# Seven of eleven gate/up panels of a SwiGLU layer with half their contraction by Strassen's block products

## The chip, the cores and the metric

The kernel runs on one core of one Trainium2 chip. The metric is the device time of one execution in microseconds (us), lower is better. The kernel before takes 2181.07 us, the median of three runs (2180.75, 2181.07, 2186.59). Engines are named as in the profile: PE is TensorE's matmuls and PEld its weight loads, DVE is VectorE, ACT is ScalarE, POOL is GpSimd, SP is SyncE, whose queue issues the DMAs.

## What is computed

A trunk of two layers over 256 tokens of width 2048, in float32. Each layer has a mixer (layer 0: a linear recurrence beside spatial gating; layer 1: stick-breaking attention beside pooling) and a SwiGLU feed-forward part, each followed by a LayerNorm, with scales, shifts and gates that come from a conditioning vector c (adaLN). What matters here is the feed-forward part of layer 1:

```python
D_FF = 5632
def swiglu(h, w_gate, w_up, w_down):
    return (jax.nn.silu(h @ w_gate) * (h @ w_up)) @ w_down
...
h = x * (1.0 + scale2) + shift2
ffn_out = swiglu(h, ffn_w_gate[layer], ffn_w_up[layer], ffn_w_down[layer])
x = layer_norm(ALPHA * x + (1.0 + gate2) * ffn_out, norm_g[layer, 1], norm_b[layer, 1])
```

## The kernel before, in words

The 256 tokens are two blocks of 128 (`tb`). The contraction over 2048 is cut into four chunks of 512 (`ch`), each of four k-tiles of 128. The 5632 columns of gate and up are cut into eleven panels of 512. A weight is a tile of 128 x 2048 numbers (1 MB): one chunk of the contraction, one panel, gate or up. `load_raw` (line 139) loads it on SP's queue into one of four raw buffers named w.

Products are made at nearly full float32 precision from two parts. `split` (line 81) lets ACT write the upper part h (line 84, a copy that rounds) and DVE the lower part l = w - h (line 85), in halves of 128 x 1024; h and l have four buffers each, so two weights. The activations xs are split in the same way, once, into xh and xl (four chunks of 128 x 4 x 256). `products` (line 154) then runs three matmuls of 512 columns per k-tile: xh h, xh l and xl h (lines 161 to 163). A weight thus gives 2 blocks x 4 k-tiles x 3 = 24 matmuls, and a half gives 12. They add up in PSUM banks named acc, of which there are six; two more, aux, take transposes.

`linear` (line 181) goes through groups of weights: for each group over the chunks, for each chunk over the group's weights, loading, splitting and multiplying. In `ffn` (line 384) a group is one panel with its gate and its up, so a panel takes 8 weights and four banks, and after the last chunk `evac_gu` (line 393) lets ACT take silu of the gate's bank (line 398) and DVE multiply it by the up's bank (line 406); the product is transposed on PE (line 228) and copied into hid by ACT or DVE (line 412). In layer 1 all eleven panels run like that. After each of the first four groups `resid` prepares a part of the residual on DVE (`residual`, lines 370 to 376) from rows of norm_g and norm_b that lie in the row buffers rg and rb, one buffer each. Then `rows` (line 231) loads the rows of the layer's last LayerNorm into the same buffers, `gate_rows` (line 240) spreads the gate, and the down-projection runs, a `linear` over hid, whose chunks are split as they come (xh, xl), and w_down.

After each weight `linear` calls a pump. It issues work of the adaLN terms that are still to come: a pump of rate 0.2 issues a unit at each fifth call. A unit is a load of 1 MB into one of the four raw buffers and two DVE instructions of 128 x 1024 that multiply and add up (`ada_dot`, line 94, line 99). In the feed-forward part of layer 1 the pump named last has rate 0.2 and 16 units.

No order is written out by hand here. A scheduler orders the instructions of each engine when the kernel is built, by their place in the program and by when they can start, and a tile waits for a free buffer of its name; on the chip each engine then runs its instructions in that order.

Of the kernel before, what the change touches and what calls it, by code (L numbers as in the profile page):

```python
# [10 lines left out]
ALU = mybir.AluOpType  # L11
# [17 lines left out]
RAW_GA = (0, 1)  # L29
RAW_OUT = (0, 1)  # L30
PAD = 16

_VEC = {}
_off = 0
# [8 lines left out]
def trunk_kernel(ctx, tc, I, out):  # L43
# [134 lines left out]
    def acc_bank():  # L178
        return psum["acc"].tile([P, NB], F32, name="acc")

    def linear(groups, chunks, wsrc, stat, evac, after=None, pump=None, opened=None, close=None,
               raw=None):
        ng, nch = len(groups), len(chunks)
        total = ng * nch
        for gi, group in enumerate(groups):
            banks = opened if gi == 0 and opened is not None else {}
            for ci, ch in enumerate(chunks):
                first, last = ci == 0, ci == nch - 1
                left = total - gi * nch - ci
                if first and banks:  # L190
                    if last:
                        for tb in range(2):
                            for nb in group:
                                evac(nb, tb, banks[nb, tb])
                    continue
                if close is not None and left == QUIET and pump is not None:
                    drain(pump.gen)
                st = stat(gi, ch)
                if close is not None and left == 1:
                    close(group, {nb: load_w(wsrc(nb, ch)) for nb in group}, banks, st, evac)  # L200
                    break
                for nb in group:
                    xr = raw(gi, ci, nb) if raw is not None else None
                    hl = load_w(wsrc(nb, ch)) if xr is None else load_raw(wsrc(nb, ch))
                    flush(mark["v"])
                    for hf in range(2):
                        for tb in range(2):
                            if first and hf == 0:
                                banks[nb, tb] = acc_bank()
                            if xr is None:  # L210
                                products(banks[nb, tb], st, hl, tb, (hf,), first, last)
                            else:
                                products32(banks[nb, tb], xr, hl, tb, (hf,), first, last)
                    if last:
                        for tb in range(2):
                            evac(nb, tb, banks[nb, tb])
                    if pump is not None and not (close is not None and left <= QUIET):
                        pump()
            if after is not None:
                after(gi)  # L220
# [4 lines left out]
    def transposed(src, n):  # L225
        pt = psum["aux"].tile([P, n, P], F32, name="aux")
        for i in range(n):
            T.transpose(pt[:, i], src[:, i * P:(i + 1) * P], ident)  # L228
        return pt

    def rows(l, s):
        rg = p_row.tile([P, D], F32, name="rg")
        nc.sync.dma_start(rg, I["norm_g"][l, s:s + 1, :].partition_broadcast(P))
        rb = p_row.tile([P, D], F32, name="rb")
        nc.sync.dma_start(rb, I["norm_b"][l, s:s + 1, :].partition_broadcast(P))
        return rg, rb
# [141 lines left out]
    def ffn_src(l):  # L378
# [2 lines left out]
            return (I["wu"] if up else I["wg"])[l, pan, ch]  # L381
        return src

    def ffn(l, ln, resid, x, pump, passes, finish):
        xs = ln["xs"]
        with tc.tile_pool(name=f"hid{l}", bufs=1) as p_hid:
            hid = p_hid.tile([P, FF // P, S], F32, name="hid")
            sil = {}

            def slot(pan):  # L390
                return pan if passes is None else (pan - 1) % NPAN

            def evac_gu(nb, tb, bk, part=None):
                pan, up = divmod(nb, 2)
                if not up:
                    sg = p_t.tile([P, NB], F32, name=f"sg{tb}")
                    if part is None:
                        A.activation(sg, bk, AF.Silu)
                    else:
                        V.tensor_tensor(sg, part, bk, op=ALU.add)  # L400
                        A.activation(sg, sg, AF.Silu)
                    sil[tb] = sg
                    return
                sg = sil[tb]
                if part is None:
                    V.tensor_tensor(sg, sg, bk, op=ALU.mult)
                else:
                    V.tensor_tensor(part, part, bk, op=ALU.add)
                    V.tensor_tensor(sg, sg, part, op=ALU.mult)
                pt = transposed(sg, 4)  # L410
                h0 = 4 * slot(pan)
                nc.any.tensor_copy(hid[:, h0:h0 + 4, tb * P:(tb + 1) * P], pt)

            src = ffn_src(l)
            p0 = 0
            if passes is not None:
                p0 = 5
                groups = [(2 * p, 2 * p + 1) for p in range(p0)]

                def part(nb, tb):  # L420
                    return hid[:, 4 * nb + 2 * tb:4 * nb + 2 * tb + 2].rearrange("p a b -> p (a b)")

                def stash(nb, tb, bk):
                    A.activation(part(nb, tb), bk, AF.Copy)

                def add(nb, tb, bk):
                    V.tensor_tensor(part(nb, tb), part(nb, tb), bk, op=ALU.add)  # L427

                def final(nb, tb, bk):
                    evac_gu(nb, tb, bk, part(nb, tb))  # L430

                for ch in range(4):
                    linear(groups, (ch,), src, lambda gi, c: xs[c], (stash, add, add, final)[ch],
                           pump=passes[ch] if ch < 3 else pump, opened=ln["banks"] if ch == 0 else None)
                    if ch < 3:
                        drain_all(passes[ch])
            linear([(2 * p, 2 * p + 1) for p in range(p0, NPAN)], range(4), src, lambda gi, ch: xs[ch], evac_gu,
                   after=lambda gi: resid(gi) if gi < 4 else None, pump=pump,
                   opened=ln["banks"] if p0 == 0 else None)
            rg, rb = rows(l, 1)  # L440
            gate_rows(l, 1)
            stats = [p_t.tile([P, 4, 6], F32, name=f"st{tb}") for tb in range(2)]
            res, close = finish(stats, rg, rb)
            linear([(0, 1), (2, 3)], range(NPAN), lambda nb, ch: I["wd"][l, nb, ch],
                   lambda gi, ch: xs_split(hid[:, 4 * slot(ch):4 * slot(ch) + 4]), make_resid(x, (l, 1), stats),
                   pump=pump, close=close)
        return res
# [467 lines left out]
```

## Time and profile before

| | |
|---|---|
| time, median of three runs | 2181.07 us |
| span of the profiled execution | 2175.9 us |
| median less span | 5.2 us |
| PE, DVE, ACT busy, share of the span | 97%, 74%, 44% |
| feed-forward part of layer 1, panels 4 to 10 | 1607 to 1919 us |

The profile is of one execution. It shows the span from its first instruction to its last; of the profiled execution itself no other time is given, and the runs' times, taken without a profile, lie about 5 us above the span. Busy times add up the instructions' durations; those of matmuls are modelled and overlap, and so do the ends of DVE's instructions by some hundredths of a microsecond. In rows of groups, "L85 DVE TENSOR_TENSOR l<-w,h 128x1024 ... x113" are the instructions of line 85 on DVE that read tiles w and h and write tile l. In a timeline, "[1.50 <-ACT h L84]" says that the engine stood idle for 1.50 us before, until line 84's writing of h on ACT released it.

### The profile page before, as it was taken

To read this page: it belongs to the slowest core of one execution; us is meant where nothing else is said; L and a number is where in the kernel's file an instruction comes from. 1 tells how busy PE (TensorE), PEld (TensorE's weight loads), DVE (VectorE), ACT (ScalarE), POOL (GpSimd) and SP (SyncE) were. 2 spreads that over 40 slices of the span, in tenths; PEclk is the share of its full clock that TensorE was granted. 3 is DMA by queue.
4 is the path that set the end of the run, shared out by engine and by line. 5 is a ranking of instruction groups with operands and counts; after the bars stand their busy time and mean duration, and the time that the engine had idled before them with its cause. 6 is when DMAs were issued, how large, how long until landed. Compare 5 with 4: busy or idle time off the path is not lost.

```text
span 2175.9 us, 24074 instructions
## 1 busy us (share of the span) xinstructions
PE 2111.6 (97%) x9124; PEld 1666.4 (77%) x9124; DVE 1618.6 (74%) x2202; ACT 966.5 (44%) x1124; POOL 31.5 (1%) x55
## 2 busy tenths in 40 slices
PE   7989999999999999999999999999999999999996
PEld 3556767887888888888868777868888888888885
DVE  7778988899977788889779977666555555555656
ACT  1215733544544445444444556354444444444442
POOL 0000000000000000000000011000000000000000
PEclk9999999999999999999999999999999999999998
DMA  9987787988888888888858877646676666555552
GB/s 399 388 322 267 303 329 297 341 325 336 301 314 312 322 330 322 335 319 312 319 217 311 324 267 292 261 173 221 230 271 229 222 226 233 208 203 193 194 194 91
DMA packets 84747, 601.20 MB, mean 276 GB/s; under 512 B 9444, under 2 KB 9876, under 8 KB 13846
## 3 DMA queue, kind: packets, MB, share of 16 engines
q1 hardware_dynamic: 84630, 599.67, 73.7%
q8 instruction: 71, 1.16, 0.2%
q14 instruction: 46, 0.37, 0.1%
HBM read 597.51 MB, written 2.12 MB: 276 GB/s over the span
## 4 chain that ended last, share of the span: by engine, by line
PE 85%; DVE 9%; ACT 2%; DMA 2%; issue 1%; POOL 1%; SPq 0%; DVEq 0%; ACTq 0%; POOLq 0%
PE acc L162 25%; PE acc L163 25%; PE acc L161 24%; DVE w L99 3%; PE hd L547 3%; PE acc L152 3%; DVE l L85 2%; PE aux L228 2%; DMA w<-in_ada_w 1%; PE hs L162 1%; PE hs L163 1%; PE hs L161 1%; DMA w<-in_w_cd 0%; ACT h L84 0%; POOL z L736 0%
## 5 line engine op out<-in xcount | busy, mean ns | idle before, releaser
L85 DVE TENSOR_TENSOR l<-w,h 128x1024 fp32r<-128x1024 f32 x676 | 822.9, 1223 | 421.4 <-ACT h L84 420.1
L84 ACT ACTIVATE h<-w 128x1024 fp32r<-128x1024 f32 x676 | 711.6, 1059 | 862.0 <-PE acc L163 689.4
L162 PE MATMUL acc<-l,xh 128*128 128x512 f32 x2608 | 1019.2, 391 | 6.2 <-DVE l L85 5.8
L161 PE MATMUL acc<-h,xh 128*128 128x512 f32 x2608 | 1018.2, 392 | 5.9 <-ACT xh L318 4.5
L163 PE MATMUL acc<-h,xl 128*128 128x512 f32 x2608 | 1018.3, 391 | 0.0
L162 PEld LDWEIGHTS acc<-l,xh 128*128 128x128 f32 x2608 | 489.8, 188 | 112.4 <-DVE l L85 11.8
L161 PEld LDWEIGHTS acc<-h,xh 128*128 128x128 f32 x2608 | 489.5, 188 | 108.2 <-ACT xh L318 5.5
L163 PEld LDWEIGHTS acc<-h,xl 128*128 128x128 f32 x2608 | 489.8, 188 | 100.4 <-DVE xl L319 0.3
L99 DVE SCALAR_TENSOR_TENSOR w<-w,silc 128x1024 f32<-128x1024 f32 x384 | 459.0, 1219 | 18.0 <-DMA w<-in_ada_w 15.6
L547 PE MATMUL hd<-w,y 128*128 128x512 f32 x192 | 93.8, 642 | 20.7 <-DVE y L545 20.7
L547 PEld LDWEIGHTS hd<-w,y 128*128 128x128 f32 x192 | 38.4, 205 | 72.7 <-issue 43.2
L85 DVE TENSOR_TENSOR xl<-hid,xh 128x1024 fp32r<-128x1024 f32 x44 | 53.9, 1224 | 34.2 <-ACT xh L84 33.6
L84 ACT ACTIVATE xh<-hid 128x1024 fp32r<-128x1024 f32 x44 | 46.8, 1063 | 63.0 <-PE acc L162 63.0
L152 PE MATMUL acc<-w,hx 128*128 128x512 f32 x96 | 43.1, 599 | 2.8 <-ACT hx L313 2.7
L161 PE MATMUL hs<-h,xh 128*128 128x512 f32 x96 | 40.9, 428 | 0.0
L162 PE MATMUL hs<-l,xh 128*128 128x512 f32 x96 | 39.0, 406 | 0.0
L163 PE MATMUL hs<-h,xl 128*128 128x512 f32 x96 | 38.0, 396 | 0.0
L84 ACT ACTIVATE xh<-y 128x1024 fp32r<-128x1024 f32 x12 | 12.7, 1058 | 56.6 <-DVE y L545 48.6
L152 PEld LDWEIGHTS acc<-w,hx 128*128 128x128 f32 x96 | 17.6, 190 | 23.4 <-issue 17.5
L99 DVE DVE_READ_ACCUMULATOR w<-w,silc 128x1 f32 x384 | 31.3, 82 | 0.0
L152 PE MATMUL acc<-w,y 128*128 128x512 f32 x64 | 28.5, 592 | 0.0
L427 DVE TENSOR_TENSOR hid<-hid,acc 128x512 f32<-128x512 f32 x40 | 27.2, 683 | 1.5 <-PE acc L163 1.4
(207 smaller groups left out, 851.4 us busy)
## 6 DMA issues: line engine op xcount, KB each, us to landing
w<-in_ada_w SPq DMA_DIRECT2D x192, 1024.0 KB, 5.1
w<-in_wg SPq DMA_DIRECT2D x88, 1024.0 KB, 5.2
w<-in_wu SPq DMA_DIRECT2D x88, 1024.0 KB, 5.1
w<-in_wd SPq DMA_DIRECT2D x88, 1024.0 KB, 4.9
w<-in_w_cd SPq DMA_DIRECT2D x32, 1024.0 KB, 6.2
w<-in_w_ab SPq DMA_DIRECT2D x20, 1024.0 KB, 5.2
w<-in_w_ab_out SPq DMA_DIRECT2D x16, 1024.0 KB, 7.0
w<-in_w_cd_out SPq DMA_DIRECT2D x16, 1024.0 KB, 6.7
```

Source lines behind the costliest of these rows:

```text
L84: A.activation(h, src, AF.Copy)
L85: mark["v"] = V.tensor_tensor(l, src, h, op=ALU.subtract)
L99: V.scalar_tensor_tensor(w[:, cs], w[:, cs], 1.0, silc[:, cs], op0=ALU.mult, op1=ALU.mult, accum_out=acc[:, hf:hf + 1])
L152: T.matmul(bk, x[:, k, ts], w[:, k], start=first and k == 0, stop=last and k == 3)
L161: T.matmul(bk, xh[:, k, ts], h[:, j], start=first and k == 0, stop=False)
L162: T.matmul(bk, xh[:, k, ts], l[:, j], start=False, stop=False)
L163: T.matmul(bk, xl[:, k, ts], h[:, j], start=False, stop=last and k == 3)
L228: T.transpose(pt[:, i], src[:, i * P:(i + 1) * P], ident)
L427: V.tensor_tensor(part(nb, tb), part(nb, tb), bk, op=ALU.add)
L547: T.matmul(banks[nb, tb], xt[:, k, tb * P:tb * P + P], w[:, i // 2], start=kb == 0, stop=kb == KB - 1)
```

## The change

Layer 1's panels 0 to 3 stay as they are (`FOLD = 4`). Panels 4 to 10 go to a new function `folded`. For chunks 0 and 1 it takes the two token blocks and two chunks as a 2 x 2 block matrix of x, and gate and up of the two chunks as a 2 x 2 block matrix of weights, and forms the four results with Strassen's seven block products (in Winograd's form) instead of eight. Block sums of x are made and split once, ahead of panel 4. Sums of weights are made in each panel by four DVE instructions of 128 x 2048 (`plus` and the sum into t), and each sum is split like a weight. Chunks 2 and 3 run as before (`plain`). Seven banks and partial results are joined by DVE sums of 128 x 512. One of the eight loads (b22) goes into the row buffer rb, t lies in the row buffer rg. `BY_DMA` is empty, so no sum is made by a DMA. The pump is called eight times per panel, as before.

```diff
+FOLD = 4
+BY_DMA = ()
...
+    def product(bk, st, hl, first, last=False):
+        xh, xl = st
+        for hf in range(2):
+            h, l = hl[hf]
+            for j in range(2):
+                k = 2 * hf + j
+                T.matmul(bk, xh[:, k], h[:, j], start=first and k == 0, stop=False)
+                T.matmul(bk, xh[:, k], l[:, j], start=False, stop=False)
+                T.matmul(bk, xl[:, k], h[:, j], start=False, stop=last and k == 3)
+
+    def folded(p_s, src, pans, xs, pump, emit):
...
+        sx = [p_s.tile([P, 3, CH, P], F32R, name=n) for n in ("sxh", "sxl")]
...
+        tmp = p_row.tile([P, 4, CH, P], F32, name="rg")
+        a21, a11, s, a = (tmp[:, i] for i in range(4))
+
+        def put(st, v):
+            A.activation(st[0], v, AF.Copy)
+            V.tensor_tensor(st[1], v, st[0], op=ALU.subtract)
+
+        x11, x12, x22 = view(0, t0), view(1, t0), view(1, t1)
+        s1, s2, s4, s3 = slot(0), slot(1), slot(2), view(0, t1)
+        V.tensor_tensor(a21, *s3, op=ALU.add)
+        V.tensor_tensor(a11, *x11, op=ALU.add)
+        V.tensor_tensor(a, *x22, op=ALU.add)
+        V.tensor_tensor(s, a21, a, op=ALU.subtract)
+        put(s1, s)
+        V.tensor_tensor(s, s, a11, op=ALU.subtract)
+        put(s2, s)
+        V.tensor_tensor(a, *x12, op=ALU.add)
+        V.tensor_tensor(a, a, s, op=ALU.add)
+        put(s4, a)
+        V.tensor_tensor(a21, a11, a21, op=ALU.subtract)
+        put(s3, a21)
...
+        def plain(bks, w, c, first, last):
+            hl = halves_of(w)
+            for hf in range(2):
+                for tb in range(2):
+                    opens = first[tb] if isinstance(first, tuple) else first
+                    products(bks[tb], xs[c], hl, tb, (hf,), opens, last)
+            pump()
...
+        for pan in pans:
+            g, u = 2 * pan, 2 * pan + 1
+            b11 = load_raw(src(g, 0))
+            b12 = load_raw(src(u, 0))
+            b22 = p_row.tile([P, 4, NB], F32, name="rb")
+            nc.sync.dma_start(b22, src(u, 1))
+            w11 = halves_of(b11)
+            m1 = acc_bank()
+            product(m1, x11, w11, True, True)
+            c11 = p_t.tile([P, NB], F32, name="sg0")
+            A.activation(c11, m1, AF.Copy)
+            t = p_row.tile([P, 4, NB], F32, name="rg")
+            V.tensor_tensor(t, b11, b12, op=ALU.add)
+            m5 = acc_bank()
+            product(m5, s1, halves_of(t), True, True)
+            pump()
+            plus("t2", t, b22, src(u, 1))
+            m6 = acc_bank()
+            product(m6, s2, halves_of(t), True, True)
+            c21 = p_t.tile([P, NB], F32, name="sg1")
+            V.tensor_tensor(c21, c11, m6, op=ALU.add)
+            c12 = t512()
+            V.tensor_tensor(c12, m5, c21, op=ALU.subtract)
+            be, bd = acc_bank(), acc_bank()
+            plain((be, bd), load_raw(src(u, 2)), 2, True, False)
+            b21 = load_raw(src(g, 1))
+            bb = acc_bank()
+            product(bb, x12, halves_of(b21), True)
+            pump()
+            plus("t3", b12, b22, src(u, 1))
+            m7 = acc_bank()
+            product(m7, s3, halves_of(b12), True, True)
+            V.tensor_tensor(c21, c21, m7, op=ALU.add)
+            c22 = t512()
+            V.tensor_tensor(c22, c12, m7, op=ALU.subtract)
+            ba = acc_bank()
+            plain((bb, ba), load_raw(src(g, 2)), 2, (False, True), False)
+            product(be, s4, halves_of(b22), False)
+            pump()
+            plus("t4", t, b21, src(g, 1))
+            plain((be, bd), load_raw(src(u, 3)), 3, False, True)
+            V.tensor_tensor(c12, c12, be, op=ALU.add)
+            V.tensor_tensor(c22, c22, bd, op=ALU.add)
+            product(ba, x22, halves_of(t), False)
+            pump()
+            plain((bb, ba), load_raw(src(g, 3)), 3, False, True)
+            for tb, (sg, up, bk) in enumerate(((c11, c12, bb), (c21, c22, ba))):
+                V.tensor_tensor(sg, sg, bk, op=ALU.add)
+                A.activation(sg, sg, AF.Silu)
+                V.tensor_tensor(sg, sg, up, op=ALU.mult)
+                emit(pan, tb, sg)
...
-            linear([(2 * p, 2 * p + 1) for p in range(p0, NPAN)], range(4), src, lambda gi, ch: xs[ch], evac_gu,
+            p1 = FOLD if l else NPAN
+            linear([(2 * p, 2 * p + 1) for p in range(p0, p1)], range(4), src, lambda gi, ch: xs[ch], evac_gu,
                    after=lambda gi: resid(gi) if gi < 4 else None, pump=pump,
                    opened=ln["banks"] if p0 == 0 else None)
+            if p1 < NPAN:
+                folded(p_hid, src, range(p1, NPAN), xs, pump, emit)
```

`halves_of` splits a weight as `load_w` does, `plus` is a sum of two tiles of 128 x 2048 on DVE, and `emit` is the transposing and copying into hid that `evac_gu` did at its end.

## Rows read from the trace of the kernel before

**Rows 1.** The page: the span, and busy time of each engine
```profile
span 2175.9 us, 24074 instructions
...
PE 2111.6 (97%) x9124; PEld 1666.4 (77%) x9124; DVE 1618.6 (74%) x2202; ACT 966.5 (44%) x1124; POOL 31.5 (1%) x55
```

**Rows 2.** Timeline of DVE: start us, us, engine, line, operation, out<-in, count
```profile
1607.08 1.28 DVE L406 TENSOR_TENSOR sg<-sg,acc 128x512 f32<-128x512 f32 x2
...
1918.62 1.28 DVE L406 TENSOR_TENSOR sg<-sg,acc 128x512 f32<-128x512 f32 x2
```

**Rows 3.** Windows: stretch, its length, busy us of each engine, PEclk, DMA share, GB/s
```profile
1607.10:1651.60 44.50, 44.50 (x201) 36.83 (x201) 26.13 (x31) 18.65 (x19) 0.00 (x0) 1.00 0.73 261
1607.10:1918.60 311.50, 311.50 (x1401) 257.70 (x1401) 175.30 (x182) 133.93 (x137) 0.00 (x0) 1.00 0.62 226
```

**Rows 4.** Waits from 1607 to 1919 us: us in total, times, longest us
```profile
ACT h L84 <- PE acc L163: 162.5, 102, 1.7
DVE l L85 <- ACT h L84: 132.4, 94, 2.0
```

**Rows 5.** Groups by form, 1607 to 1919 us: busy us, mean ns, idle before
```profile
L161 PE MATMUL acc<-h,xh 128*128 128x512 f32 x450 | 175.7, 391 | 0.0
L163 PE MATMUL acc<-h,xl 128*128 128x512 f32 x449 | 175.4, 391 | 0.0
L162 PE MATMUL acc<-l,xh 128*128 128x512 f32 x449 | 174.7, 389 | 0.0
L85 DVE TENSOR_TENSOR l<-w,h 128x1024 fp32r<-128x1024 f32 x113 | 138.4, 1224 | 132.4 <-ACT h L84 132.4
...
L99 DVE SCALAR_TENSOR_TENSOR w<-w,silc 128x1024 f32<-128x1024 f32 x20 | 23.8, 1218 | 0.0
L406 DVE TENSOR_TENSOR sg<-sg,acc 128x512 f32<-128x512 f32 x15 | 9.6, 679 | 0.0
...
L412 DVE COPY hid<-aux 128x512 f32<-128x512 f32 x6 | 4.2, 692 | 0.9 <-PE aux L228 0.8
L85 DVE TENSOR_TENSOR xl<-hid,xh 128x1024 fp32r<-128x1024 f32 x3 | 3.7, 1225 | 3.8 <-ACT xh L84 3.8
L99 DVE DVE_READ_ACCUMULATOR w<-w,silc 128x1 f32 x20 | 1.6, 81 | 0.0
```

**Rows 6.** The chain in order of time: the eight transposes of panel 4
```profile
1652.47 0.49 PE aux L228 x4
...
1653.20 0.44 PE aux L228 x4
```

**Rows 7.** Timeline of DVE: steps between instructions that follow without a wait
```profile
1561.45 1.22 DVE L85 TENSOR_TENSOR l<-w,h 128x1024 fp32r<-128x1024 f32 x1
1562.59 1.28 DVE L406 TENSOR_TENSOR sg<-sg,acc 128x512 f32<-128x512 f32 x2
1563.78 1.22 DVE L99 SCALAR_TENSOR_TENSOR w<-w,silc 128x1024 f32<-128x1024 f32 x1
1564.93 0.08 DVE L99 DVE_READ_ACCUMULATOR w<-w,silc 128x1 f32 x1
...
1598.92 1.29 DVE L375 TENSOR_TENSOR x<-x,rg 128x512 f32<-128x512 f32 x2
1600.12 1.29 DVE L376 TENSOR_TENSOR x<-x,rb 128x512 f32<-128x512 f32 x2
1601.33 1.22 DVE L85 TENSOR_TENSOR l<-w,h 128x1024 fp32r<-128x1024 f32 x1
```

**Rows 8.** Windows: the two stretches in which DVE is fullest
```profile
490.00:544.00 54.00, 53.26 (x230) 42.47 (x229) 53.47 (x80) 23.21 (x29) 0.00 (x0) 1.00 0.89 336
544.00:600.00 56.00, 56.00 (x265) 45.93 (x265) 54.49 (x76) 32.27 (x39) 0.00 (x0) 1.00 0.81 301
```

**Rows 9.** Waits from 490 to 544 us
```profile
PEld acc L162 <- DVE l L85: 2.9, 5, 0.7
...
PE acc L162 <- DVE l L85: 0.4, 2, 0.2
```

**Rows 10.** Waits from 544 to 600 us
```profile
DVE sg L400 <- PE acc L163: 0.7, 2, 0.5
DVE l L85 <- ACT h L84: 0.3, 1, 0.3
```

**Rows 11.** DMA issues: engine, operation, count, KB each, median us to landing
```profile
w<-in_wg SPq DMA_DIRECT2D x88, 1024.0 KB, 5.2
w<-in_wu SPq DMA_DIRECT2D x88, 1024.0 KB, 5.1
...
rg<-in_norm_g SPq DMA_DIRECT2D x4, 1024.0 KB, 7.3
rb<-in_norm_b SPq DMA_DIRECT2D x4, 1024.0 KB, 6.9
```

**Rows 12.** Timeline of SP: issues of the last LayerNorm's rows
```profile
1600.23 0.33 SPq L233 DMA_DIRECT2D rg<-in_norm_g  x1
...
1605.34 0.42 SPq L235 DMA_DIRECT2D rb<-in_norm_b  x1
```

**Rows 13.** Timeline of DVE: the first reader of the last norm_g row
```profile
2159.24 1.40 DVE L837 SCALAR_TENSOR_TENSOR x<-x,mv,rg 128x512 f32<-128x512 f32 x2
```

**Rows 14.** Timeline from 1660 to 1663 us: an upper part and its lower part
```profile
1661.21 1.06 ACT L84 ACTIVATE h<-w 128x1024 fp32r<-128x1024 f32 x1 [1.66 <-PE acc L163]
...
1662.30 1.23 DVE L85 TENSOR_TENSOR l<-w,h 128x1024 fp32r<-128x1024 f32 x1 [1.50 <-ACT h L84]
```

**Rows 15.** Timeline of DVE: three instructions that each read the one before
```profile
2151.39 0.69 DVE L264 TENSOR_TENSOR t<-acc,gb 128x512 f32<-128x512 f32 x1 [0.40 <-PE acc L163]
2152.12 0.69 DVE L269 SCALAR_TENSOR_TENSOR x<-x,t 128x512 f32<-128x512 f32 x1
2152.84 0.69 DVE L270 BATCH_NORM_STATS2 st<-x 128x6 f32<-128x512 f32 x1
```

More of the change, by code (lines that the diff above doesn't have):

```diff
@@ L382, in ffn_src, with view, slot, halves_of @@
         return src
+    def product(bk, st, hl, first, last=False):
[9 more added lines that the diff above has]
+        sx = [p_s.tile([P, 3, CH, P], F32R, name=n) for n in ("sxh", "sxl")]
+        t0, t1 = slice(0, P), slice(P, S)
+        def view(c, ts):
+            return xs[c][0][:, :, ts], xs[c][1][:, :, ts]
+        def slot(i):
+            return sx[0][:, i], sx[1][:, i]
+        tmp = p_row.tile([P, 4, CH, P], F32, name="rg")
[17 more added lines that the diff above has]
+        put(s3, a21)
+        def halves_of(w):
+            return [split(w[:, 2 * hf:2 * hf + 2], p_h, p_l, [P, 2, NB], "h", "l") for hf in range(2)]
+        def plus(name, w, other, where):
+            if name in BY_DMA:
+                G.dma_start(w, where, accum_op=ALU.add)
+            else:
+                V.tensor_tensor(w, w, other, op=ALU.add)
+        def plain(bks, w, c, first, last):
[5 more added lines that the diff above has]
+            pump()
+        def t512():
+            return p_t.tile([P, NB], F32, name="t512")
+        for pan in pans:
[49 more added lines that the diff above has]
+                emit(pan, tb, sg)
@@ L409, in evac_gu, with emit @@
                     V.tensor_tensor(sg, sg, part, op=ALU.mult)
+                emit(pan, tb, sg)
+            def emit(pan, tb, sg):
                 pt = transposed(sg, 4)
```

## The prediction

> **What bounds the kernel now.** I read the busy shares first: TensorE (PE) is busy for 97% of the span, VectorE (DVE) for 74%, ScalarE (ACT) for 44% [rows 1]. A share over the whole span says little about the one stretch that is edited, so I took the two `L406` products that close panel 3 and panel 10 of layer 1: they start at 1607.08 and 1918.62 us, so the seven edited panels take 311.5 us, 44.5 us each [rows 2]. In that stretch PE is busy for all 311.50 us at a granted clock of 1.00, while DVE is busy for 175.30 and ACT for 133.93 [rows 3]. The reader is to see there a stage that TensorE alone sets: ACT waits for matmuls to free a buffer (162.5 us in all), DVE waits for ACT (132.4 us), and nothing of weight waits on a DMA [rows 4].
>
> So work taken from TensorE is worth its full time until another engine needs as long. The question is how far away DVE is from that.
>
> **TensorE: what is removed.** A panel has 192 split matmuls (8 weights of 24 each), 7 x 192 = 1,344, as the 1,348 of the stretch show [rows 5]. Eight transposes take 0.49 + 0.44 us [rows 6]; (44.5 - 0.93) / 192 = 0.227 us from matmul to matmul. In the first two chunks of the contraction the eight blocks (2 token blocks x gate/up x 2 chunks) of 12 matmuls become seven, so a panel loses 12 matmuls, 2.72 us; seven panels lose 84, **19.0 us**. TensorE alone would then need 292.5 us.
>
> **VectorE: what is added.** Durations overlap when instructions follow each other without a wait, so I cost by start-to-start steps. A 1024-wide subtract is followed after 1.14 us, an adaLN product after 1.15; two 512-wide instructions take 1.19 to 1.21 [rows 7]. I take 1.145 and 0.60. The sums of weights are 2048 wide and no such instruction is in the trace: the two steps differ by 0.545 us for 512 elements, so 0.60 + 3 x 0.545 = 2.235 us. Bounds: 2.18 (four times 0.545, no fixed part) and 2.40 (four times 0.60).
>
> Per panel: the weights to be split become 11 instead of 8 (b11, three states of t, b21, the sum in b12 and b22 for the seven products, four plain ones), so 22 subtracts, 25.2 us; four weight sums, 8.9 us; ten 512-wide sums and products of results, two of them in the place of `L406`, 6.0 us. That is 40.1 us, 280.9 for seven panels. The adaLN products stay at their rate: 20 in the stretch [rows 5], 22.9 us. Six of the copies into hid fall to DVE there [rows 5], 3.6 us. The sums of x, once: eight sums and four splits of 512, 7.2 us; they write the row buffer that holds norm_g until the last residual part, so they can't start before its two instructions end, at 1601.33 [rows 7]. Panel 3's own closing products and copy come behind that, 1.8 us.
>
> The sum: 280.9 + 22.9 + 3.6 + 7.2 + 1.8 = **316.4 us** of VectorE from 1601.33 on, so it ends at 1917.7 if it never waits. Before, the closing pair that starts at 1918.62 ends some 1.2 us later, at 1919.8. VectorE without one idle moment thus ends 2.1 us sooner than before, and TensorE's 19 us are not to be had: **DVE takes over as the bound, almost exactly where PE stood.**
>
> **How much DVE will wait.** The trace has two stretches in which DVE was about as full: from 490 to 544 us it was busy for 53.47 of 54, from 544 to 600 for 54.49 of 56 (durations, with their overlaps), and TensorE lost 0.74 us in the first and nothing in the second [rows 8]. In the first, PE waited for lower parts for 0.4 us [rows 9]; in the second, DVE waited for PE and ACT for 1.0 us [rows 10], 1.8% of it. The order in which the instructions stand on each engine, which is drawn up when the kernel is built, can thus keep DVE full. The new panels are tighter: the chain sum (DVE), upper part (ACT), lower part (DVE), product (PE), result (DVE) goes back and forth more often, h and l have four buffers, and the four raw weight buffers hold b12 and b21 for half a panel. I take a little more than that share, 7 us in 312. The floor is 0. Net: -2.1 + 7 = **+5 us**.
>
> **What else moves.** ACT gets six more upper parts and one copy of a bank per panel, some 7 us on the 18.65 that it is busy now [rows 3]: 26 of 44, covered by its own idle time. The weights are the same eight loads of a megabyte per panel, landing in 5.1 to 5.2 us [rows 11]; one goes to the row buffer rb instead of a raw buffer, and none is added, as no sum goes by DMA. SP's queue gets them in another order, and behind them the two rows for the last LayerNorm, issued now at 1600.23 and 1605.34 [rows 12], move back until t and b22 give up their buffers, near 1915; they land in about 7 us [rows 11] and are first read at 2159.24 [rows 13], so 240 us of down-projection hide them, and without that cover they would cost those 7 us. The gate's row waits for nothing new. Banks: eight accumulators go through six buffers per panel; m1, m5 and m6 are given back by ACT and DVE before m7 and ba need one. If DVE is late there, PE waits in its place, which is the same lateness and not a second one. The added waits on DVE (c21 for m6, c22 for m7, c12 and c22 for be and bd) have the next weights' splits queued behind them, and PE waits for those. Behind panel 10 the down-projection finds fewer splits done in advance: before, three xl [rows 5] and as many halves as h and l have buffers, four, were ready; a new start with one xl and one half, 2.3 us, lies beside PE's last 24 matmuls (5.4 us), so I take 0, with 3 as the upper bound.
>
> **A rule weighed.** From row to row DVE starts the next instruction 0.08 us before the profile lets the last one end: a subtract of 1.22 to 1.23 us is followed after 1.14 [rows 7]. The Trainium skill, "VectorE: DVE Perf Modes", section "The DRAIN you can't avoid", says that the next operation does not start before the pipeline has emptied and that chaining does not get round this. By that rule nothing could be counted at its step, and the sum would be that of the last case below.
>
> **The rivals.**
>
> *Slower: the sums are not covered.* After each of three sums per panel (t, t plus b22, b12 plus b22) the lower part must wait until ACT has made the upper one. That takes 1.06 us on ACT, and DVE starts 0.03 us behind it [rows 14], so about 1.1 us. It is hidden only if another weight or a result is ready just then. If it never is: 21 x 1.1 = 23 us, less the 2.1: +21 us, **2202 us**, and with the other waits of the forecast up to 2208. It decides from the point at which more than a third of these gaps (7 of 21, 8 us) stay open. For it speaks that raw buffers are scarce just there, against it the two full stretches [rows 9, 10].
>
> *Faster: TensorE stays the bound.* If the ten adaLN units (22.9 us) drift behind panel 10, DVE needs 293.5 us, about TensorE's 292.5. Then most of the 19.0 us stays: 4 us for the start, 15 gained, **2166 us**. For it: their gate is only needed in the down-projection, where DVE is less loaded. Against it: each holds a raw buffer from its load on, and the calls that issue them keep their places and their rate.
>
> *Slower: no overlap between instructions.* Where one needs what the one before it wrote, the overlap is gone: 512-wide instructions of 0.69 us then follow each other after 0.73 and 0.72 [rows 15]. If it were so everywhere, whole durations [rows 5] would count, 2048-wide ones at 1.224 + 2 x 0.545 = 2.31: 7 x (22 x 1.224 + 4 x 2.31 + 10 x 0.68) = 300.8 us, adaLN 25.4, copies 4.2, sums of x 8.2, panel 3's end 2.1, in all 340.7, 24 us more than the sum: **2210 us**. The steps of 1.14 and 0.60 stand against it [rows 7]: splits, which are most of the work, don't read each other.
>
> That the change doesn't remove the matmuls is no case: their number is fixed in the code.
>
> **How the numbers follow.** The sum is made against the profiled span of 2175.9 us; the median of the three runs, 2181.07, lies 5.2 above it, and I carry that. 2175.9 + 5 + 5.2 = **2186 us**. Under 0.3% (6.5 us) a measurement of this kernel can't be told from no change. Chances: forecast 0.58, uncovered sums 0.25, TensorE stays the bound 0.14, no overlap 0.03. Within the forecast the bounds are: below, no idle time (-2.1), the cheapest 2048-wide sums (28 x 0.055 = 1.5) and all copies on ACT (3.6), so -7, 2174 us; above, the dear sums (28 x 0.165 = 4.6), the start of the down-projection (3) and somewhat more waiting, +15, 2196. Of its 0.58, 0.43 lies within 0.3%, 0.12 above and 0.03 below. Faster is 0.14 + 0.03 = 0.17, same 0.43, slower 0.12 + 0.25 + 0.03 = 0.40. The range takes in the forecast and the uncovered sums, 2174 to 2208, and leaves the faster case and the last one out; the forecast's own is 2174 to 2196.
>
> **What would show it.** In the changed profile: 84 matmuls fewer; DVE busy by its steps for nearly the whole stretch; panels of 44 to 47 us; PE waiting for the lower parts (l), several us per panel, where it waited for nothing. If PE is busy throughout and panels take 42 us, DVE's sum is wrong. If DVE shows some 20 gaps of a microsecond behind the sums, ended by ACT, it is the first rival. If PE waits for raw weights' DMA, the held buffers were mis-sized, which I cost at nothing of its own.

## The result, and the profile after

The changed kernel takes 2207.78 us (median of 4 runs, 2203.52 to 2208.43), the kernel before 2182.78 us beside it (4 runs, 2180.75 to 2186.59): a ratio of 1.0107, 95% interval 1.0089 to 1.0125. It is **25.0 us slower**. The forecast was 2186 us; its range of 2174 to 2208 holds the result by 0.2 us, at the end that belongs to a rival; the forecast's own range, 2174 to 2196, doesn't hold it.

The page of the changed kernel, which answers to [rows 1]:

```profile
span 2206.2 us, 24135 instructions
...
PE 2114.3 (96%) x9040; PEld 1660.7 (75%) x9040; DVE 1760.3 (80%) x2334; ACT 1018.8 (46%) x1183; POOL 30.8 (1%) x55
```

PE has the 84 matmuls less (9124 to 9040) and yet is busy for longer, 2114.3 us for 2111.6. Something makes matmuls longer.

Where the time lies is read from DVE's sums that close panels 3, 4 and 10 (line 524 is the `L406` of before, line 497 the closing sum of a new panel), as [rows 2]:

```profile
1612.32 0.68 DVE L524 TENSOR_TENSOR sg<-sg,acc 128x512 f32<-128x512 f32 x1
...
1664.53 1.50 DVE L497 TENSOR_TENSOR sg<-sg,acc 128x512 f32<-128x512 f32 x2
...
1948.64 1.28 DVE L497 TENSOR_TENSOR sg<-sg,acc 128x512 f32<-128x512 f32 x2
```

The seven panels take 1948.64 - 1612.32 = 336.3 us in place of 311.5: **24.8 us more**, the whole difference of the medians. Panel 4 takes 52.2 us and the six after it 284.1, 47.4 each, where all took 44.5. Behind panel 10 nothing changes: 2206.2 - 1948.64 = 257.6 us, before 2175.9 - 1918.62 = 257.3. The start lies 5.2 us later than in [rows 2], but so it does, for the most part, in another profiled execution of the old panels (1610.84, experiment 8): that is scatter between executions.

Windows of the changed kernel, columns as in [rows 3] (after the length: busy us of PE, PEld, DVE, ACT, POOL; PEclk; DMA): panel 4, the six later panels, then panels 6 and 8, and two pieces of panel 8.

```profile
1612.30:1664.50 52.20, 45.76 (x191) 36.06 (x190) 50.28 (x48) 27.32 (x29) 0.00 (x0) 0.90 0.50 183
1664.50:1948.60 284.10, 265.07 (x1131) 213.82 (x1130) 263.96 (x261) 157.82 (x165) 0.00 (x0) 0.96 0.58 215
...
1713.00:1757.90 44.90, 41.84 (x186) 33.80 (x185) 42.70 (x43) 25.78 (x27) 0.00 (x0) 1.00 0.57 212
...
1806.00:1854.10 48.10, 43.92 (x189) 35.44 (x188) 44.92 (x45) 25.84 (x27) 0.00 (x0) 0.96 0.59 213
...
1814.00:1816.00 2.00, 0.00 (x0) 0.00 (x0) 2.00 (x2) 0.77 (x1) 0.00 (x0) 1.00 0.00 0
...
1818.00:1820.00 2.00, 2.00 (x6) 1.52 (x6) 2.00 (x3) 1.13 (x2) 0.00 (x0) 0.50 0.88 365
```

Before, PE was busy for all of the stretch at a granted clock of 1.00. Now PE has holes, and its clock is 0.96 in the mean: in panel 8, 0.50 of full speed, the level of 1.2 GHz, behind 2 us in which it ran nothing. Panel 6, whose clock stays at 1.00, is 3.2 us shorter than panel 8, of which 1.1 us are shorter idle times of PE (3.06 us for 4.18).

Waits of the changed kernel from 1607 to 1950 us, as [rows 4] (us in all, times, longest):

```profile
ACT h L86 <- PE acc L165: 86.7, 53, 1.9
...
ACT h L86 <- DVE rg L437: 19.4, 7, 4.9
PE acc L392 <- ACT h L86: 18.0, 7, 4.5
DVE l L87 <- ACT h L86: 12.2, 20, 1.3
...
PE acc L393 <- DVE l L87: 6.0, 9, 1.5
...
PE acc L163 <- ACT h L86: 1.4, 1, 1.4
```

PE, which waited for nothing, waits 18.0 us for upper parts, once per panel, and 6.0 for lower parts. With the 1.4 us of the last row that is 25.4 us. ACT's waits for line 437 also come once per panel: it is the sum `t2`, t plus b22.

Groups by form, changed kernel, 1612 to 1950 us, as [rows 5]: matmuls of the Strassen products with blocks of x itself (xh) and with sums of x (sxh), and two of the sums that are 2048 wide.

```profile
L393 PE MATMUL acc<-l,xh 128*128 128x512 f32 x112 | 43.7, 390 | 0.0
...
L393 PE MATMUL acc<-l,sxh 128*128 128x512 f32 x84 | 38.7, 461 | 6.1 <-DVE l L87 6.0
...
L437 DVE TENSOR_TENSOR rg<-rg,rb 128x2048 f32<-128x2048 f32 x7 | 16.0, 2290 | 0.1
L462 DVE TENSOR_TENSOR rg<-w 128x2048 f32<-128x2048 f32 x7 | 16.0, 2288 | 0.4 <-DMA w<-in_wu 0.2
```

The same matmul takes 461 ns in the mean where it multiplies x sums, 390 elsewhere: the slow clock sits at the openings of the panels, where most of these products (the fifth and the sixth) stand.

One opening, panel 8, in the timeline of all engines (start us, us, engine, line):

```profile
1806.34 1.06 ACT L86 ACTIVATE h<-rg 128x1024 fp32r<-128x1024 f32 x1 [1.67 <-PE acc L165]
...
1807.16 2.28 DVE L437 TENSOR_TENSOR w<-w,rb 128x2048 f32<-128x2048 f32 x1
...
1809.37 1.28 DVE L499 TENSOR_TENSOR sg<-sg,t 128x512 f32<-128x512 f32 x2
...
1810.57 1.21 DVE L87 TENSOR_TENSOR l<-rg,h 128x1024 fp32r<-128x1024 f32 x1
...
1811.70 1.22 DVE L101 SCALAR_TENSOR_TENSOR w<-w,silc 128x1024 f32<-128x1024 f32 x1
...
1812.85 2.29 DVE L437 TENSOR_TENSOR rg<-rg,rb 128x2048 f32<-128x2048 f32 x1
1812.86 0.40 PE L394 MATMUL acc<-h,sxl 128*128 128x512 f32 x1
1815.05 1.22 DVE L101 SCALAR_TENSOR_TENSOR w<-w,silc 128x1024 f32<-128x1024 f32 x1
1815.23 2.00 ACT L86 ACTIVATE h<-rg 128x1024 fp32r<-128x1024 f32 x2 [3.10 <-DVE rg L437]
...
1816.32 2.36 DVE L87 TENSOR_TENSOR l<-rg,h 128x1024 fp32r<-128x1024 f32 x2
...
1816.34 0.50 PE L392 MATMUL acc<-h,sxh 128*128 128x512 f32 x1 [3.08 <-ACT h L86]
...
1817.60 0.80 PE L393 MATMUL acc<-l,sxh 128*128 128x512 f32 x1 [0.76 <-DVE l L87]
...
1818.19 0.63 PE L394 MATMUL acc<-h,sxl 128*128 128x512 f32 x1
```

This is the mechanism. The fifth product m5 ends on PE at 1813.3. The sixth needs t2, and t2 is a chain across engines: the second half of t's lower part (1810.57), the sum (1812.85, as it overwrites t in the buffer rg), the upper part on ACT (1815.23), the product (1816.34), then its lower part (1816.32 to 1817.60). That lower part is late itself: its upper part was done at 1807.4, but on DVE the sum in b12 (1807.16) and panel 7's closing products (1809.37) stand ahead of it. An adaLN product that nobody is in a hurry for stands in the chain at 1811.70. Another at 1815.05, ahead of t2's lower part, costs next to nothing, as the upper part is done only at 1816.3. PE stands for 3.08 us, runs one matmul, stands for 0.76, and then its matmuls follow at 0.43 us instead of 0.23. In panel 4 the long wait is one product earlier, ahead of the fifth, as t itself is late there (experiment 5).

### The profile page after: what moved, and what is told of

Its sections match the earlier page's. It is cut to its first block, busy times and chain, and to the rows that moved or that the text cites. A ratio compares the mean times of both kernels' runs of the same rounds, so it can differ in the third digit from the quotient of the medians.

```text
span 2206.2 us, 24135 instructions
## 1 busy us (share of the span) xinstructions
PE 2114.3 (96%) x9040; PEld 1660.7 (75%) x9040; DVE 1760.3 (80%) x2334; ACT 1018.8 (46%) x1183; POOL 30.8 (1%) x55
## 5 line engine op out<-in xcount | busy, mean ns | idle before, releaser
L163 PE MATMUL acc<-h,xh 128*128 128x512 f32 x2384 | 931.5, 392 | 7.4 <-ACT xh L320 4.5
L164 PE MATMUL acc<-l,xh 128*128 128x512 f32 x2384 | 932.5, 391 | 6.1 <-DVE l L87 5.6
L165 PE MATMUL acc<-h,xl 128*128 128x512 f32 x2384 | 930.9, 391 | 0.0
L164 PEld LDWEIGHTS acc<-l,xh 128*128 128x128 f32 x2384 | 448.1, 188 | 103.6 <-DVE l L87 11.1
L163 PEld LDWEIGHTS acc<-h,xh 128*128 128x128 f32 x2384 | 447.7, 188 | 101.9 <-ACT xh L320 5.5
L165 PEld LDWEIGHTS acc<-h,xl 128*128 128x128 f32 x2384 | 447.9, 188 | 92.4 <-DVE xl L321 0.3
L86 ACT ACTIVATE h<-rg 128x1024 fp32r<-128x1024 f32 x42 | 43.7, 1058 | 44.5 <-DVE rg L437 19.4
L392 PE MATMUL acc<-h,sxh 128*128 128x512 f32 x84 | 38.7, 460 | 18.0 <-ACT h L86 18.0
L87 DVE TENSOR_TENSOR l<-rg,h 128x1024 fp32r<-128x1024 f32 x42 | 50.3, 1220 | 4.3 <-ACT h L86 3.9
L154 PE MATMUL acc<-w,hx 128*128 128x512 f32 x96 | 43.1, 599 | 2.8 <-ACT hx L315 2.7
L393 PE MATMUL acc<-l,sxh 128*128 128x512 f32 x84 | 38.7, 461 | 6.1 <-DVE l L87 6.0
L392 PE MATMUL acc<-h,xh 128*128 128x512 f32 x112 | 43.8, 391 | 0.0
L393 PE MATMUL acc<-l,xh 128*128 128x512 f32 x112 | 43.7, 390 | 0.0
L394 PE MATMUL acc<-h,xl 128*128 128x512 f32 x112 | 43.6, 390 | 0.0
```

Of the source, the lines that this page charges most:

```text
L86: A.activation(h, src, AF.Copy)
L87: mark["v"] = V.tensor_tensor(l, src, h, op=ALU.subtract)
L154: T.matmul(bk, x[:, k, ts], w[:, k], start=first and k == 0, stop=last and k == 3)
L163: T.matmul(bk, xh[:, k, ts], h[:, j], start=first and k == 0, stop=False)
L164: T.matmul(bk, xh[:, k, ts], l[:, j], start=False, stop=False)
L165: T.matmul(bk, xl[:, k, ts], h[:, j], start=False, stop=last and k == 3)
```

## The experiments

Three causes were open: PE's waits at the openings, with the slow clock behind them; VectorE's work as such, as the forecast had it; and what happens once, in panel 4. In the table "beside" is each median less that of the kernel before in its own comparison; the seven panels go from closing sum to closing sum; PE's waits add up the PE rows of the waits view; PEclk is that of panels 5 to 10.

| | median us | beside | panel 4 | panels 5-10 | PE waits | PEclk |
|---|---|---|---|---|---|---|
| changed kernel | 2207.78 | +25.0 | 52.2 | 284.1 | 25.4 | 0.96 |
| 1 adaLN early | 2190.95 | +11.8 | 54.0 | 266.7 | 17.6 | 1.00 |
| 2 sum off the chain | 2195.32 | +16.1 | 52.5 | 271.7 | 19.9 | 0.99 |
| 3 filler | 2195.72 | +16.5 | 52.3 | 275.8 | 9.3 | 1.00 |
| 4 u2 between | 2188.97 | +9.8 | 51.8 | 266.8 | 16.1 | 0.99 |
| 5 x sums early | 2200.42 | +18.8 | 45.8 | 284.5 | 20.6 | 0.96 |
| 6 moves 1, 4 and 5 | 2167.67 | -14.0 | 43.3 | 252.0 | 0 | 1.00 |
| 7 as 6, t2 in its own buffer | 2163.41 | -18.2 | 43.3 | 251.6 | 0 | 1.00 |
| 8 kernel before, adaLN early | 2182.03 | +0.4 | 44.5 | 267.0 | 0 | 1.00 |
| 9 moves 4 and 5 | 2185.60 | +3.6 | 43.1 | 270.4 | 11.1 | 0.98 |
| 10 as 5, t2 in its own buffer | 2189.35 | +7.3 | 42.4 | 278.7 | 14.6 | 0.96 |

**1. adaLN early.** The remaining adaLN steps are issued at a higher rate, so that they are done ahead of panel 4.

```diff
-    last = Pump(units(1, G2), 0.2)
+    last = Pump(units(1, G2), 0.5)
```

> The last pump runs at rate 0.5 instead of 0.2, so all 16 adaLN units are done in panels 0 to 3, where VectorE is half idle, and none is left for the folded panels: 22.9 us less VectorE work there, nothing else changed. WORK (VectorE's total sets the seven panels): about 20 us faster, near 2186 us. CHAIN (TensorE's wait for the second sum of each panel and the slow clock behind it set them): only the products that stood inside that chain go, 3 to 8 us faster, 2200 to 2205 us. CLOCK alone: the gaps stay, so the stretches at half clock stay, as CHAIN.

Measured 2190.95 us, ratio 1.0055 (1.0037 to 1.0073). Windows of this kernel, panel 4 and the six later ones:

```profile
1610.60:1664.70 54.10, 45.68 (x190) 35.97 (x189) 50.51 (x51) 27.33 (x29) 0.00 (x0) 0.91 0.49 178
1664.70:1931.40 266.70, 257.46 (x1132) 206.54 (x1131) 243.64 (x219) 157.45 (x165) 0.00 (x0) 1.00 0.52 193
```

The time beside the kernel before falls by 13 us, from 25.0 to 11.8: more than the 3 to 8 us that were expected of a shorter chain, less than the 20 of DVE's work. DVE is relieved by 263.96 - 243.64 = 20.3 us in the six panels, PE's clock stays at 1.00, and they become 17.4 us shorter. It can't be told from this run alone whether that is DVE's work or the chain. Panel 4 keeps its loss.

**2. Sum off the chain.** The sum t plus b22 goes into a buffer that nobody reads; the sixth product and t4 take t as it is.

```diff
-            plus("t2", t, b22, src(u, 1))
+            gt = p_row.tile([P, 4, NB], F32, name="gb")
+            V.tensor_tensor(gt, t, b22, op=ALU.add)
```

> The sum t + b22 is still made, at the same length, but into the idle row buffer gb, and nobody reads it: m6 takes t again, and the last sum adds b21 to t without b22. So part of the computation is left out (b22 in two of the seven products), VectorE's work is the same, and only the chain split of t, sum, upper part, lower part is broken. WORK: no change, 2203 to 2210 us. CHAIN with the clock: the waits of TensorE behind the sum (18 of the 25 us) and most of the 17 to 19 us at half clock go, until VectorE's work limits: 2180 to 2190 us.

Measured 2195.32 us, ratio 1.0072 (1.0055 to 1.0089). DVE does the same work and the panels are 336.3 - 324.2 = 12.1 us shorter. So DVE's work alone didn't set the changed kernel's time. But the time lies between the two forecasts, and PE's waits fall only from 25.4 to 19.9 us: that chain isn't all of it either.

**3. Filler.** Twelve matmuls that nobody reads stand between the fifth and the sixth product.

```diff
             plus("t2", t, b22, src(u, 1))
+            fill = psum["aux"].tile([P, NB], F32, name="aux")
+            for _ in range(12):
+                T.matmul(fill, xs[2][0][:, 0, t0], xs[3][0][:, 0:2], start=True, stop=True)
```

> Twelve matmuls per panel whose result nobody uses (2.7 us of TensorE each panel, 19 us in all) stand between m5 and m6, where TensorE waits. Nothing is taken away. CLOCK (a good part of the loss is matmuls at half clock behind the gap): the granted clock stays at 1.00 in most panels and the time falls by 8 to 15 us, to 2193 to 2200 us, although TensorE has more to do. CHAIN without a clock effect: the fillers fit into gaps of 3 to 4 us, no change, 2205 to 2210 us. WORK: no change or up to 5 us slower.

Measured 2195.72 us, ratio 1.0076 (1.0061 to 1.0091). Windows, panel 4 and the six later ones:

```profile
1608.50:1660.70 52.20, 47.34 (x203) 37.58 (x202) 50.24 (x48) 27.33 (x29) 0.00 (x0) 0.97 0.48 182
1660.70:1936.50 275.80, 271.27 (x1203) 221.06 (x1202) 263.16 (x261) 157.68 (x165) 0.00 (x0) 1.00 0.60 222
```

This gives PE back as many matmuls as the change removes, 84 or 19.1 us of work, and the panels become 8.3 us **shorter**. DVE and ACT run the same instructions in the same order in the seven panels. If only the length of the holes counted, filling them with unread work could at best change nothing. What is gained is the clock: 1.00 in place of 0.96. By the timelines PE takes 49 steps of about 0.43 us from matmul to matmul in the seven panels of the changed kernel, and 5 here.

**4. u2 between.** The plain quarter of up's third chunk, 24 matmuls that need no sum, moves from behind the sixth product to before it. The order alone changes.

```diff
             pump()
+            be, bd = acc_bank(), acc_bank()
+            plain((be, bd), load_raw(src(u, 2)), 2, True, False)
             plus("t2", t, b22, src(u, 1))
...
-            be, bd = acc_bank(), acc_bank()
-            plain((be, bd), load_raw(src(u, 2)), 2, True, False)
```

> The same instructions in another program order: the plain weight of up, chunk 2 (24 matmuls, 5.4 us, no sum in it) stands between m5 and m6 instead of behind m6. WORK: the same VectorE work, 2203 to 2208 us. CHAIN with the clock: TensorE has 5.4 us to do while VectorE makes the sum and ScalarE its upper part, so the wait for m6 and the half clock behind it go: 20 to 28 us faster, 2180 to 2188 us.

Measured 2188.97 us, ratio 1.0042 (1.0027 to 1.0057), 1 us above the range of CHAIN: the six later panels lose 17.3 us at the same work, panel 4 keeps its loss. In all four runs that loss stands, 51.8 to 54.0 us against 44.5. The six later panels:

```profile
1663.20:1930.00 266.80, 257.14 (x1126) 206.67 (x1125) 261.45 (x260) 153.91 (x165) 0.00 (x0) 0.99 0.61 230
```

DVE is now busy for 261.45 of 266.80 us, 98%, and the panels take what they took before the change, 267.0 us. With the hole at the second sum covered, DVE is nearly the bound that the forecast saw.

**5. x sums early.** Panel 4's hole is the longest. The x sums write into rg, which the residual part reads; they start behind it, at 1607.04 us, and t follows them there. The timeline of PE in the changed kernel:

```profile
1616.60 0.40 PE L394 MATMUL acc<-h,xl 128*128 128x512 f32 x1
1621.53 0.79 PE L392 MATMUL acc<-h,sxh 128*128 128x512 f32 x1 [4.54 <-ACT h L86]
1623.85 0.80 PE L393 MATMUL acc<-l,sxh 128*128 128x512 f32 x1 [1.52 <-DVE l L87]
1624.44 0.63 PE L394 MATMUL acc<-h,sxl 128*128 128x512 f32 x1
```

Two holes of 4.54 and 1.52 us, and behind them steps at half clock. Here the x sums get the buffer gb and stand behind panel 1; only the last split stays, as it overwrites x.

```diff
-        tmp = p_row.tile([P, 4, CH, P], F32, name="rg")
+        tmp = p_row.tile([P, 4, CH, P], F32, name="gb")
...
+                if l and gi == 1:
+                    sums["x"] = x_sums(p_hid, xs)
```

> The same work as the changed kernel; the x sums of the folded stretch are made beside panels 1 to 3 of the layer, in a buffer of their own, and only the last of them is split behind panel 3. Theory GAP (PE's waits at the openings of panels and the half clock behind them make the loss): the 7.7 us that panel 4 costs over a panel of before, with its gap of 7 us in PE, go for the most part (panel 4 at 45 to 48 us in place of 52.2), and the six later panels stay near 47.4: 4 to 8 us under the changed kernel, 2200 to 2204. Theory VECTOR (VectorE's work alone sets the end): the 7 us of x sums leave the stretch that VectorE bounds, so the gain is spread over all seven panels and is 7 to 10 us, and the later panels come down to about 46.

Measured 2200.42 us, ratio 1.0084 (1.0069 to 1.0099):

```profile
1612.00:1657.70 45.70, 43.73 (x188) 35.29 (x187) 42.58 (x40) 24.68 (x25) 0.00 (x0) 0.96 0.54 207
1657.70:1942.20 284.50, 265.78 (x1131) 214.16 (x1130) 263.86 (x262) 157.81 (x165) 0.00 (x0) 0.96 0.58 215
```

As GAP has it: panel 4 falls to 45.8 us, and the later panels keep their 47.4. 7 us less work for DVE gave the later panels nothing.

**6. Three moves.** The edits of 1, 4 and 5 together.

> The same work as the changed kernel, with three moves together: x sums beside panels 1 to 3, adaLN's remaining steps done earlier (rate 0.5 in place of 0.2), and the plain u2 quarter between the fifth and sixth products. Theory GAP: with no wait left at the openings PE sets the pace again at full clock: 42 to 43.5 us a panel, 294 to 304 us for the seven against 311.5 before, which makes 2165 to 2178, faster than the kernel before by 3 to 16 us. Theory VECTOR: VectorE has 40 us a panel without adaLN and copies, and some idle time that no order takes away: 44 to 45 us a panel, 2178 to 2188, not faster than before.

Measured 2167.67 us (6 runs, 2164.36 to 2172.71), ratio 0.9934 (0.9918 to 0.9950): 14.0 us **faster than the kernel before**. Windows:

```profile
1614.50:1657.80 43.30, 43.30 (x194) 35.26 (x193) 42.32 (x42) 24.62 (x26) 0.00 (x0) 1.00 0.59 220
1657.80:1909.80 252.00, 252.00 (x1123) 205.44 (x1122) 238.88 (x218) 154.37 (x165) 0.00 (x0) 1.00 0.55 204
```

PE is busy throughout at 1.00 again, and a panel takes 42.0 us; the forecast's TensorE alone was 292.5 / 7 = 41.8. The waits, 1614 to 1910 us:

```profile
ACT h L86 <- PE acc L165: 56.1, 36, 1.7
ACT h L86 <- DVE rg L439: 27.3, 7, 4.1
...
DVE l L87 <- ACT h L86: 13.7, 13, 1.2
```

ACT's wait for the second sum (line 439 here) hasn't gone; it is longer than before, 27.3 us for 19.4. But there is no row of PE left: the plain quarter runs over it. A wait costs what is not covered, not what it measures.

**7. Own buffer, on top of 6.** t2 gets the buffer gb, so that it doesn't overwrite t.

```diff
-            plus("t2", t, b22, src(u, 1))
+            t2 = p_row.tile([P, 4, NB], F32, name="gb")
+            V.tensor_tensor(t2, t, b22, op=ALU.add)
+            t = t2
```

> As the kernel with three moves, and the second weight sum t2 is written to a buffer of its own, so that it need not wait until the splits of t have been read. Theory GAP: if the second sum waiting for the splits of t (ScalarE's upper part read of the same buffer) is still a wait that PE sees, 1 to 5 us come off; if the plain quarter between the products hides it already, the same within 1.5 us. Theory VECTOR: no change, the work of VectorE being the same.

Measured 2163.41 us (6 runs, 2161.12 to 2171.03), ratio 0.9919 (0.9902 to 0.9935). ACT's wait for the sum falls from 27.3 us to one of 2.5 us:

```profile
ACT h L86 <- PE acc L394: 20.3, 61, 0.8
...
ACT h L86 <- DVE gb L471: 2.5, 1, 2.5
```

and the seven panels take 294.9 us for 295.3. The intervals of 6 and 7 overlap; that the 4 us between their medians are real isn't shown, and their panels don't hold them.

**8. A control.** The kernel before with the edit of 1.

> The kernel before with only adaLN's remaining steps done earlier (rate 0.5 in place of 0.2), no Strassen panels in layer 1: a control. If the gain that the same edit had in the changed kernel (17 us) comes from the openings of the Strassen panels, it is worth nothing here: 2177 to 2185, the same as the kernel before. If the order of adaLN is worth something in itself, over 6 us faster.

Measured 2182.03 us (10 runs), ratio 1.0000 (0.9987 to 1.0013). The place of adaLN is worth something only where DVE is on PE's path.

**9. Two moves.** The edits of 4 and 5, adaLN left in place.

> The x sums beside panels 1 to 3 and the plain u2 quarter between the fifth and sixth products, with adaLN's steps left where the changed kernel has them. Theory ADDS (each move takes away its own wait, and adaLN's steps in VectorE's chain are a wait of their own): the sum of what the two moves gave alone, 2189.0 less 7.4, so 2179 to 2184, no faster than the kernel before. Theory GAP alone (with a product's worth of other work behind the fifth product, PE never runs dry, whatever VectorE does between): as with the three moves, 42 to 43 us a panel, 2164 to 2172.

Measured 2185.60 us (10 runs), ratio 1.0018 (1.0005 to 1.0030). The six later panels:

```profile
1655.30:1925.70 270.40, 259.76 (x1126) 208.52 (x1125) 261.65 (x260) 154.03 (x165) 0.00 (x0) 0.98 0.61 227
```

GAP alone fails here, ADDS holds within 2 us. With adaLN in the stretch DVE is busy for 261.65 of 270.40 us, 97%, and PE waits again. Here too VectorE is, nearly, the bound that the forecast saw. So adaLN's place is needed for the gain of 6; whether one of the other two moves could be spared wasn't run.

**10. Own buffer without the other order.** The edit of 7 on the kernel of 5.

> The x sums beside panels 1 to 3, and the second weight sum in a buffer of its own; order and adaLN as in the changed kernel. Theory BUFFER (the second sum is late because it overwrites t, and so waits for the splits of t): 1.1 to 2.2 us of each panel's opening goes, and some of the half clock behind it, 1 to 3 us a panel: 2182 to 2194, against 2200.4 with the x sums alone. Theory CHAIN (the length of the chain t, second sum, upper part, lower part sets the wait, with the buffer or without): within 3 us of 2200.4.

Measured 2189.35 us, ratio 1.0036 (1.0020 to 1.0052). The time lies in BUFFER's range. Against 5 the seven panels become 330.3 - 321.1 = 9.2 us shorter, 1.3 us each, near the lower end of the 1 to 3 expected: where nothing covers the chain, the overwriting of t is a good part of it. On top of 6 it was worth nothing.

## Why the prediction was right and wrong

**What held.** The 84 matmuls went, and they were worth their price: experiment 6 runs the same matmuls without a hole in 295.3 us, against the 292.5 that were worked out. The 2048-wide sums follow in 2.20 us (1812.85 to 1815.05), inside the bounds of 2.18 to 2.40, 0.03 under the 2.235 taken. The copies went to ACT, all 14. The down-projection's start cost nothing (257.6 us for 257.3), and of waits for a raw weight's DMA there is 0.2 us.

**The sum of VectorE held too, but alone it was not what set the end.** The first x sum, and the first instruction behind DVE's work for panel 10:

```profile
1607.04 0.68 DVE L417 TENSOR_TENSOR rg<-xh,xl 128x512 f32<-128x512 f32 x1
...
1952.34 1.22 DVE L87 TENSOR_TENSOR l<-w,h 128x1024 fp32r<-128x1024 f32 x1
```

Of these 345.3 us DVE stood idle for some 22, by its timeline. The rest, 323, is the 316.4 less 3.6 for the copies, with 8.0 for seven splits of the down-projection (four xl, three l), which the sum had left out of the stretch, and some 2 that aren't accounted for. That this work set the changed kernel's time is contradicted by experiments 2, 3 and 4: the same DVE work or more, and 8 to 18 us less in the panels. But that TensorE's 19 us "are not to be had" beside it was borne out. In experiments 4 and 9, with PE's holes partly covered, DVE is 98% and 97% busy in the six later panels, and of the runs with adaLN's steps in the stretch none is faster than the kernel before.

**The step that failed is "How much DVE will wait".** It took 7 us, and some 22 were seen. It went by two stretches in which DVE was full and PE lost almost nothing [rows 8]. In those stretches no weight is a sum of others: each lower part needs only its own loaded weight and upper part. A new panel has a chain, and one product of 12 matmuls, 2.7 us, as all the cover over it. The text listed the chain and still priced it by stretches that have none. Worse, it put the idle time on DVE's account only, as if PE's wait were always "the same lateness", as it says of the banks. PE's account shows where the time went: against the 295.3 us without holes, 336.3 - 295.3 = 41.0 us are lost, 25.4 in waits and 15.6 in the rest, of which some 10 us are the 49 steps of about 0.43 us, at half clock. The 16.2 that experiment 6 gains on 311.5, less 41.0, is the -24.8 that was seen.

**The second omission is the clock.** The text read it as 1.00 [rows 3] and carried it on. Holes of 2 to 5 us in PE weren't foreseen, so neither was their price. By experiment 3, filling them paid for 19.1 us of matmuls and 8.3 us beside.

**The one-time loss.** That the x sums can't start before the residual part lets go of rg was seen, and costed as work (7.2 us) on DVE; that PE has nothing to do until they are through was not. Experiment 5 puts panel 4's own loss at 6.4 us.

**The rivals.** "The sums are not covered" gave 2202, up to 2208, and the result lies there. Its sign, some 20 gaps of a microsecond on DVE behind the sums, isn't in the trace. DVE waits for upper parts 20 times, but mostly for those of loaded weights (groups by form, 1612 to 1950 us):

```profile
L87 DVE TENSOR_TENSOR l<-w,h 128x1024 fp32r<-128x1024 f32 x99 | 117.3, 1219 | 8.5 <-ACT h L86 8.3
L87 DVE TENSOR_TENSOR l<-rg,h 128x1024 fp32r<-128x1024 f32 x42 | 50.3, 1220 | 4.3 <-ACT h L86 3.9
```

For the sums in rg it is 3.9 us, with three waits of 1.2 us by the timeline, all at second sums; and no wait for the sum in b12 is among the waits. What counts is one gap per panel on PE, in six of the seven panels at the second sum, and the slow clock behind it. So this rival had the right place and a wrong price that happened to come out near, and that the range held the result is luck. "TensorE stays the bound" named adaLN's drift behind panel 10, 2166 us: with adaLN's steps out of the stretch (done ahead of it), and with the two other moves, 2167.67 were measured. Experiment 1 shows that adaLN's place alone doesn't do it. "No overlap between instructions" falls: steps of 1.13 to 1.15 us stand in the rows of panel 8. The 5.2 us carried from span to median were mostly a quick profiled execution: here the profiled run's 2207.86 us lie 1.7 above its span.

## What to carry to other kernels

When work is taken from the engine that sets the pace and put as sums on another, add up both engines, but then walk through the longest chain that a single product waits for, and count the matmuls that are ready to run meanwhile; a stretch of the old kernel in which that other engine was full says nothing of it. Before giving such a change up, move independent products into the hole, move work without a due time out of the chain, and give a sum its own buffer: the same arithmetic went from 25 us slower to 14 to 18 us faster.

## What was not expected of the hardware

A hole in PE cost more than its length, in all 15.6 us beside 25.4. In panel 8 PE stood for 3.08 us, ran a matmul, stood for 0.76, and then ran at a granted clock of 0.50, with 0.43 us from matmul to matmul, for some 3 us; in panel 6 it stood for 2.05 and 0.76 us and the clock remained 1.00. The Trainium skill, "TensorE: Matmul & The Clock Gate", section "HAM oscillation — how this bites in real kernels", tells of a kernel in which PE runs dry in every turn of its loop, waiting for DMA, and starts each turn at half clock. This trace agrees with the pattern in panel 8 (0.50 in the window above) and not in panel 6 (1.00), with a chain over VectorE and ScalarE in the place of the DMA. And matmuls that nobody reads made the kernel faster, by 8.3 us in the seven panels.
